# Own tiles for the output halves, and the gate's pieces dealt out anew between the samples' SSD step and their attention

## The chip, the cores and the metric

The kernel runs on one core of a Trainium2 chip. Its engines are TensorE (PE; its weight loads are shown as PEld), VectorE (DVE), ScalarE (ACT), GpSimd (POOL) and SyncE (SP), whose queue issues nearly all transfers here. Each engine works through its own instructions in order; semaphores hold an instruction back until what it reads is there and the buffer that it writes is free. The metric is the device time of one execution in microseconds (us), less is better.

## The reference

One layer of a decoder trunk on a prompt of 2048 tokens and on 8 samples of 4 tokens, d_model 1024, all in float32:

```
h = rmsnorm(x, pre_g);  u = h @ w_in          # 1024 -> 5648 columns
x_lru, g_lru, q, k, v, g_attn, z, xbc, dt_raw = split(u)
y_lru  = rg_lru(causal_conv(x_lru)) * silu(g_lru)          # 512 wide
y_attn = dilated_window_attention(q, k, v) * silu(g_attn)  # 512 wide, 8 heads
y_ssd  = rmsnorm_groups(ssd(causal_conv(xbc), dt) * silu(z)) * ssd_norm_g   # 1024 wide
out = x + rmsnorm(concat(y_lru, y_attn, y_ssd) @ w_out, post_g)
```

The samples continue from caches of keys and values and from an SSD state of 8 x 16 x 64 x 128 numbers, which is read, updated and written back. The new states are outputs too.

## The kernel before

**Products.** Each product with the large weights is made three times over, as high x high, high x low and low x high parts of both operands (`mm3`, L82 to L84). So one column tile of 128 output features over 512 tokens is 8 x 3 = 24 matmuls.

**Stages.** In order: values, keys, queries and the gates; the RG-LRU branch; the convolution of xbc; the SSD step of the samples (`samples`); the attention of the samples over their caches (`sample_part`, dealt out by `fills`); the attention of the prompt (16 units, `attend`); and last the chunkwise SSD of the prompt (`ssd_part`, 16 chunks of 128 tokens) together with the output projection (`out_chunk`, the same 16 chunks, and one for the samples after the eighth).

**The gate z.** Its 1024 columns are eight tiles of 128 (`z_tile`), and a tile is five pieces of 512, 512, 256, 288 and 512 tokens. A piece is 24 matmuls into one of four PSUM buffers (tag "mm"), one SiLU on ACT into one of two buffers zo (L605), and one transfer to the DRAM scratch d_z (L606). A tile begins with the load of its weights (L143), a scaling on POOL (L146), and the split on ACT and DVE (L147, L148). Tiles 0 to 5 are the generator `zs`, 30 pieces, which serve as filler: `samples` yields 20 times and `fills` 80 times, and at some of these points one piece is drawn. What is left over is drawn at the end of `fills`. Tiles 6 and 7 follow in `z_end`, ten pieces, interleaved with the first scores of the prompt's attention. The table preload and all the attention's exponentials on ACT are held behind the last SiLU of `z_end`.

**The samples' SSD step.** For each of two groups there are two rounds of four samples. A round loads four states (tag "h0", two buffers of four states, L793), transposes them on PE (L798), copies them on ACT (L800), multiplies (L804), forms the update on PE (L808, PSUM tag "mm"), adds it on DVE (L810) and writes the states back (L815).

**The chunks.** `out_chunk(c)` makes 32 steps of three matmuls: with 8 row blocks of w_out for the halves 0 and 1, then with the other 8 blocks for both. The first 8 blocks take the RG-LRU and attention outputs, loaded as ym; the other 8 take `chunks[c]`, the high and low parts of the normalised SSD output, which `ssd_part(c)` left. `ssd_part` has 15 steps for each chunk, of which about one is drawn after every two steps of `out_chunk`, so that chunk c + 1 of the SSD runs under chunk c of the output and ends about a quarter into its own. Its steps for each of the two groups g: the decay matrix (load sg, L697 to L700), the transposed x (L710), the products yd and yo (L1251, L1256), the sum y (L1264 to L1267), the squares for the norm (ACT L721, POOL L722 and L723), the update of the state hT, then the sum over partitions on PE (rs, L726), the scaling L730, and the split into sh and sl (L1288, L1289).

**The buffers around the change.** Pool `ck` has two buffers for each tag. The SSD's y (L1264) and the finished output halves ot (L1459, L1460, sent by L1461) share the tag "yt", so they take turns on two buffers; each chunk takes four in the order y of group 0, y of group 1, ot of half 0, ot of half 1, where the y of group 1 of the next chunk comes right behind the two ot. sh and sl are tiles of all 8 blocks, two buffers each.

**Order.** The framework's planner sets each engine's order of instructions: it goes by the place in the program and by its own estimate of when the inputs are ready and buffers free, so an instruction can stand earlier or later than the program has it. On the chip the order is fixed.

Of the kernel before, what the change touches and what calls it, by code (L numbers as in the profile page):

```python
# [8 lines left out]
F32 = mybir.dt.float32  # L9
F32R = mybir.dt.float32r  # L10
AF = mybir.ActivationFunctionType
OP = mybir.AluOpType
# [20 lines left out]
def tile_hybrid_step(ctx: ExitStack, tc: tile.TileContext, A):  # L33
    nc = tc.nc
    act, dve, pool, pe, sp = nc.scalar, nc.vector, nc.gpsimd, nc.tensor, nc.sync
# [45 lines left out]
    def mm3(out, wh, wl, xh, xl, start, stop):  # L81
        pe.matmul(out, lhsT=wh, rhs=xh, start=start, stop=False)  # L82
        pe.matmul(out, lhsT=wh, rhs=xl, start=False, stop=False)  # L83
        pe.matmul(out, lhsT=wl, rhs=xh, start=False, stop=stop)  # L84
# [517 lines left out]
    def z_tile(pl, m):  # L602
        def evac(ps, t0, n):
            zt = pl.tile([128, 512], F32, tag="zo", name="zo", bufs=2)
            z_last.append(act.activation(out=zt[:, :n], in_=ps[:, :n], func=AF.Silu))  # L605
            sp.dma_start(out=d_z[128 * m:128 * m + 128, t0:t0 + n], in_=zt[:, :n])  # L606
        yield from project_steps(C_Z + 128 * m, evac, order=[CHUNKS[i] for i in (2, 1, 3, 4, 0)])
# [124 lines left out]
    def load_z(ck, c, g):  # L732
        return load_rows4(ck, c, g, "zt", d_z)
# [3 lines left out]
    zs = (None for m in range(6) for _ in z_tile(zo, m))  # L737


    with tc.tile_pool(name="cks", bufs=1) as ck:  # L740
        ps = {"t": (psT, "tp"), "y": (psG, "g")}
# [84 lines left out]
                sp.dma_start(out=d_ys[512 * g:512 * g + 512].rearrange("(j p) t -> p j t", p=128), in_=y)  # L826
                yield

        for _ in samples():
            next(zs, None)  # L830

    with tc.tile_pool(name="sa", bufs=1) as sa:
        evac_n = [0]
# [122 lines left out]
                yield  # L956

        for i, _ in enumerate(fills()):
            if i % 3 == 0:
                next(zs, None)  # L960
        for _ in zs:
            pass
# [3 lines left out]
    wo = {}  # L966
# [241 lines left out]
    chunks = {}  # L1208
# [25 lines left out]
    def ssd_part(c):  # L1234
        ck = ck0 if c == 0 else late["ck"]
        ps6 = {"t": (psA, "mm"), "y": (psA, "mm")} if c == 0 else late["ps6"]
        bc, gm, bt = ssd_open(c, ck, ps6, late["tri0" if c == 0 else "tri"])
        yield
        for g in range(2):
            hs = slice(8 * g, 8 * g + 8)  # L1240
            ecB = None if c == 0 else ck.tile([128, 4, 128], F32, tag="ecB", name="ecB", bufs=1)
            sg = ssd_decay(c, g, ck, gm, ecB)
            yield
            xb, xdt, xte = ssd_x(c, g, ck, ps6)
            pool.tensor_tensor(out=xb, in0=xb, in1=dF[:, 4 * g:4 * g + 4, None].to_broadcast([128, 4, 128]), op=OP.mult)
            yield
            hT = late["hT"]
            yd = psA.tile([128, 4, 128], F32, tag="mm", name="yd")
            for m in range(4):
                for e in range(2):  # L1250
                    pe.matmul(yd[64 * e:64 * e + 64, m], lhsT=xdt[:, 2 * m + e], rhs=sg[:, 2 * m + e],  # L1251
                              start=(m == 0), stop=(m == 3), skip_group_check=True)

            yo = None if c == 0 else psA.tile([128, 4, 128], F32, tag="mm", name="yo")
            for m in range(4 if c else 0):
                pe.matmul(yo[:, m], lhsT=hT[:, g, 128 * m:128 * m + 128], rhs=bc[:, 2 + g],  # L1256
                          start=(m == 0), stop=(m == 3), skip_group_check=True)
            yield
            zt = load_z(ck, c, g)
            y = ck.tile([128, 4, 128], F32, tag="yt", name="y")  # L1260
            if c == 0:
                dve.tensor_tensor(out=y, in0=yd, in1=xb, op=OP.add)
            else:
                dve.tensor_tensor(out=y, in0=yo, in1=ecB, op=OP.mult)  # L1264
                dve.tensor_tensor(out=y, in0=y, in1=yd, op=OP.add)
                dve.tensor_tensor(out=y, in0=y, in1=xb, op=OP.add)
            dve.tensor_tensor(out=y, in0=y, in1=zt, op=OP.mult)  # L1267
            yield
            norm = group_norm(ck, ps6, y, 128, dve if c == 0 else pool)
            next(norm)  # L1270
            yield
            stp = psA.tile([128, 512], F32, tag="mm", name="stp")
            pe.matmul(stp, lhsT=bt[:, g], rhs=xte.rearrange("p h d -> p (h d)"), start=True, stop=True)
            if c == 0:
                act.copy(out=hT[:, g], in_=stp)
            else:
                hv = hT[:, g].rearrange("p (h d) -> p h d", d=64)
                pool.tensor_tensor(out=hv, in0=hv, in1=dec[:, c, hs, None].to_broadcast([128, 8, 64]), op=OP.mult)
                dve.tensor_tensor(out=hT[:, g], in0=hT[:, g], in1=stp, op=OP.add)
            yield  # L1280
            for _ in norm:
                pass
            if g == 0:
                mh = ck.tile([128, 8, 128], F32R, tag="sh", name="sh")
                ml = ck.tile([128, 8, 128], F32R, tag="sl", name="sl")
                chunks[c] = mh, ml
            kk = slice(4 * g, 4 * g + 4)
            act.copy(out=mh[:, kk], in_=y)  # L1288
            dve.tensor_tensor(out=ml[:, kk], in0=y, in1=mh[:, kk].bitcast(F32), op=OP.subtract)  # L1289
            yield  # L1290

    ssd = (None for c in range(16) for _ in ssd_part(c))
# [29 lines left out]
    for i in range(16):  # L1322
# [3 lines left out]
        n = [0, 0]  # L1326
# [29 lines left out]
    ck = es.enter_context(tc.tile_pool(name="ck", bufs=2))  # L1356
# [28 lines left out]
    def out_chunk(c):  # L1385
        smp = c == 16
        t0, n = TT[c]
        if not smp:
            mh = c1.tile([128, 8, 128], F32R, tag="mh", name="mh")
            ml = c1.tile([128, 8, 128], F32R, tag="ml", name="ml")  # L1390
            for k0 in (0, 4):
                ym = load_rows4(ck, c, k0 // 4, "ym", d_y, 1)
                kk = slice(k0, k0 + 4)
                act.copy(out=mh[:, kk], in_=ym)
                dve.tensor_tensor(out=ml[:, kk], in0=ym, in1=mh[:, kk].bitcast(F32), op=OP.subtract)
        ops, ots, xres = [], [], []

        def residual(hf):
            sl = slice(512 * hf, 512 * hf + 512)
            xres.append(ck.tile([128, 512], F32, tag="x", name="xres", bufs=2))  # L1400
            src = A["x_prompt"][0, t0:t0 + n, sl] if not smp else A["x_sample"].rearrange("b l d -> (b l) d")[:, sl]
            sp.dma_start(out=xres[hf][:n], in_=src)

        def scaled(hf):

            sl = slice(512 * hf, 512 * hf + 512)
            ots.append(ck.tile([128, 512], F32, tag="yt", name="ot"))
            dve.tensor_tensor(out=ots[hf], in0=ops[hf], in1=pgB[:, sl], op=OP.mult)
            residual(hf)

# [3 lines left out]
        for hf in range(2 if smp else 0):  # L1414

            sl = slice(512 * hf, 512 * hf + 512)
            pq = psA.tile([128, 512], F32, tag="mm", name="pq")
            for k in range(4):
                for i in range(2):
                    for j in range(4):  # L1420
                        kk = 4 * j + k
# [5 lines left out]
            ps = psO.tile([128, 512], F32, tag="o", name="ops")  # L1427
# [5 lines left out]
        for hf, k in () if smp else order:  # L1433
            if cnt[hf] == 0:
                ops.append(psO.tile([128, 512], F32, tag="o", name="ops"))
            ps = ops[hf]
            sl = slice(512 * hf, 512 * hf + 512)
            h_, l_ = (mh, ml) if k < 8 else chunks[c]
            mm3(ps[:n], h_[:, k % 8, :n], l_[:, k % 8, :n], wo[k][0][:, sl], wo[k][1][:, sl],
                cnt[hf] == 0, cnt[hf] == 15)  # L1440
            cnt[hf] += 1
            yield
            if cnt[hf] == 16:
                jk = ck.tile([128, 512], F32, tag="zt", name="jk")
                act.activation(out=jk[:n], in_=ps[:n], func=AF.Square, accum_out=oss[:n, hf:hf + 1])
                if c == 15:
                    scaled(hf)
        dve.tensor_tensor(out=oss[:n, 0:1], in0=oss[:n, 0:1], in1=oss[:n, 1:2], op=OP.add)
        r = rstd_of(sm, oss[:, 0:1], DM, n, "ro")
        for hf in range(2):  # L1450
            sl = slice(512 * hf, 512 * hf + 512)
            dst = A["y_prompt"][0, t0:t0 + n, sl] if not smp else A["y_sample"].rearrange("b l d -> (b l) d")[:, sl]
            if c == 15:
                ot = ots[hf]
                dve.scalar_tensor_tensor(out=ot, in0=ot, scalar=r, in1=xres[hf], op0=OP.mult, op1=OP.add)
            else:
                residual(hf)
                ot = ck.tile([128, 512], F32, tag="yt", name="ot")
                dve.scalar_tensor_tensor(out=ot[:n], in0=ops[hf][:n], scalar=r[:n], in1=pgB[:n, sl], op0=OP.mult, op1=OP.mult)  # L1459
                dve.tensor_tensor(out=ot[:n], in0=ot[:n], in1=xres[hf][:n], op=OP.add)  # L1460
            sp.dma_start(out=dst, in_=ot[:n])  # L1461

    def last_state():
        for g in range(2):
            tp = psT.tile([128, 4, 128], F32, tag="tp", name="tpf")
            for j in range(4):
                pe.transpose(tp[:, j], hT[:, g, 128 * j:128 * j + 128], ident)
            ho = ck.tile([128, 4, 128], F32, tag="ho", name="ho", bufs=1)
            act.copy(out=ho, in_=tp)
            sp.dma_start(out=A["ssd_h_p"][0, 0, 8 * g:8 * g + 8].rearrange("(m e) p n -> (e p) m n", e=2), in_=ho)  # L1470

# [9 lines left out]
    for c in range(16):  # L1481
        k = 0
# [115 lines left out]
```

## Time and profile before

| | |
|---|---|
| median of 3 runs | 2015.51 us (2010.99 to 2017.05) |
| the profiled execution | 2012.49 us |
| its span, first to last instruction | 2010.6 us |
| PE busy | 1925.6 us (96%) |
| DVE busy | 1066.6 us (53%) |
| ACT busy | 742.7 us (37%) |
| POOL busy | 279.2 us (14%) |
| granted TensorE clock, mean | 0.990 of full speed |

The profile is that of one execution. A busy time is the time in which the engine had an instruction at work. Since matmuls overlap, the duration shown for a single matmul (0.39 us for 512 columns) is longer than the distance from one to the next. Waits are named by what ended them.

### The profile page before, as it was taken

To read this page: it belongs to the slowest core of one execution; us is meant where nothing else is said; L and a number is where in the kernel's file an instruction comes from. 1 tells how busy PE (TensorE), PEld (TensorE's weight loads), DVE (VectorE), ACT (ScalarE), POOL (GpSimd) and SP (SyncE) were. 2 spreads that over 40 slices of the span, in tenths; PEclk is the share of its full clock that TensorE was granted. 3 is DMA by queue.
4 is the path that set the end of the run, shared out by engine and by line. 5 is a ranking of instruction groups with operands and counts; after the bars stand their busy time and mean duration, and the time that the engine had idled before them with its cause. 6 is when DMAs were issued, how large, how long until landed. Compare 5 with 4: busy or idle time off the path is not lost.

```text
span 2010.6 us, 35818 instructions
## 1 busy us (share of the span) xinstructions
PE 1925.6 (96%) x14218; PEld 1569.0 (78%) x14218; DVE 1066.6 (53%) x2314; ACT 742.7 (37%) x1464; POOL 279.2 (14%) x346
## 2 busy tenths in 40 slices
PE   7999999999999999999999889999988999989998
PEld 7998888888888888887877667777756777567776
DVE  7315433434323666664223236666767676566664
ACT  6311525252422222223234235556543333333332
POOL 0100101111001111110001000000122232222221
PEclk9999999999999999999999999999999999999999
DMA  8322111111233222225377664334554434234341
GB/s 244 116 75 62 54 54 59 48 61 55 87 93 97 66 73 71 78 69 158 106 208 206 185 176 129 101 102 133 166 157 132 129 112 129 83 108 130 110 126 63
DMA packets 277106, 221.75 MB, mean 110 GB/s; under 512 B 33458, under 2 KB 233122, under 8 KB 276940
## 3 DMA queue, kind: packets, MB, share of 16 engines
q1 hardware_dynamic: 276940, 219.47, 36.2%
q8 instruction: 112, 1.84, 0.4%
q14 instruction: 54, 0.44, 0.1%
HBM read 150.55 MB, written 68.86 MB: 109 GB/s over the span
## 4 chain that ended last, share of the span: by engine, by line
PE 70%; DVE 9%; DMA 8%; ACT 6%; issue 4%; POOL 2%; SPq 1%; DVEq 0%; POOLq 0%; ACTq 0%
PE mm L82 15%; PE mm L83 15%; PE mm L84 15%; PE pt L1142 3%; DMA out_dram<-ot 2%; PE o L1178 2%; ACT sr L1114 2%; PE s L1087 2%; PE ops L83 2%; PE ops L84 2%; PE ops L82 2%; PE s L1066 1%; PE mmt L82 1%; PE mmt L83 1%; PE mmt L84 1%
## 5 line engine op out<-in xcount | busy, mean ns | idle before, releaser
L82 PE MATMUL mm<-xh,wh 128*128 128x512 f32 (+2 forms) x1600 | 563.9, 352 | 0.0
L83 PE MATMUL mm<-xl,wh 128*128 128x512 f32 (+2 forms) x1600 | 560.9, 351 | 0.0
L84 PE MATMUL mm<-xh,wl 128*128 128x512 f32 (+2 forms) x1600 | 560.2, 350 | 0.0
L82 PEld LDWEIGHTS mm<-xh,wh 128*128 128x128 f32 x1600 | 301.6, 188 | 40.7 <-issue 2.9
L83 PEld LDWEIGHTS mm<-xl,wh 128*128 128x128 f32 x1600 | 301.4, 188 | 39.8 <-issue 2.5
L84 PEld LDWEIGHTS mm<-xh,wl 128*128 128x128 f32 x1600 | 300.7, 188 | 38.7 <-issue 1.2
L146 POOL TENSOR_TENSOR wr<-wr,gC 128x1024 f32<-128x1024 f32 x40 | 78.7, 1967 | 398.1 <-DMA wr<-in_w_in_dram 351.4
L439 DVE SCALAR_TENSOR_TENSOR o<-u,ssdc,o 128x512 f32<-128x512 f32 (+1 forms) x216 | 122.8, 590 | 5.1
L148 DVE SCALAR_TENSOR_TENSOR wl<-wr,wh 128x1024 fp32r<-128x1024 f32 x40 | 48.9, 1223 | 120.4 <-ACT wh L147 120.4
L1114 ACT ACTIVATE sr<-sr,nm 128x384 f32<-128x384 f32 (+3 forms) x128 | 97.9, 771 | 23.3 <-DVE nm L1110 14.1
L619 ACT ACTIVATE o<-o 128x512 f32<-128x512 f32 (+2 forms) x60 | 33.1, 552 | 149.9 <-DVE o L439 78.0
L437 DVE TENSOR_SCALAR o<-u,ssdc 128x512 f32<-128x512 f32 (+1 forms) x72 | 47.2, 669 | 65.0 <-ACT u L419 56.8
L1025 ACT COPY ptsb<-pt 128x512 f32<-128x512 f32 x96 | 52.4, 583 | 75.4 <-PE pt L1142 75.3
L82 PE MATMUL mmt<-wh,xh 128*128 128x256 f32 (+3 forms) x272 | 79.2, 293 | 1.0 <-ACT xh L250 0.6
L695 ACT ACTIVATE ecB<-sg 64x512 f32<-64x512 f32 x60 | 37.8, 630 | 113.3 <-DVE y L1264 92.7
L84 PE MATMUL mmt<-wh,xl 128*128 128x256 f32 (+3 forms) x272 | 78.4, 289 | 0.0
L83 PE MATMUL mmt<-wl,xh 128*128 128x256 f32 (+3 forms) x272 | 77.9, 288 | 0.0
L1142 PE MATMUL pt<-ident,sr 128*128 128x128 f32 x576 | 75.2, 281 | 2.3 <-ACT sr L1114 1.8
L1142 PEld LDWEIGHTS pt<-ident,sr 128*128 128x128 f32 x576 | 63.7, 143 | 14.6 <-issue 8.8
L697 DVE TENSOR_SCALAR sg<-sg,cum 128x128 f32<-128x128 f32 (+1 forms) x256 | 70.0, 337 | 5.4 <-ACT ecB L695 5.2
L1087 PE MATMUL s<-k,q 64*32 64x256 f32 (+1 forms) x1536 | 68.9, 348 | 3.8 <-DVE mx L1075 3.2
L1091 DVE CUSTOM_DVE_ANT_0 sr<-s,bias 128x128 f32<-128x128 f32 (+3 forms) x128 | 58.8, 486 | 25.2 <-PE s L1087 24.1
(534 smaller groups left out, 3565.4 us busy)
## 6 DMA issues: line engine op xcount, KB each, us to landing
wr<-in_w_in_dram SPq DMA_DIRECT2D x40, 512.0 KB
sg<-d_cum SPq DMA_DIRECT2D x30, 512.0 KB
d_xbc<-o SPq DMA_DIRECT2D x36, 256.0 KB
x<-in_x_prompt_dram SPq DMA_DIRECT2D x32, 256.0 KB
vt<-in_cache_attn_v_dram SPq DMA_DIRECT2D x32, 256.0 KB
kc<-in_cache_attn_k_dram SPq DMA_DIRECT2D x32, 256.0 KB
xres<-in_x_prompt_dram SPq DMA_DIRECT2D x32, 256.0 KB
out_dram<-ot SPq DMA_DIRECT2D x32, 256.0 KB
```

The lines of the kernel that those rows point to most:

```text
L82: pe.matmul(out, lhsT=wh, rhs=xh, start=start, stop=False)
L83: pe.matmul(out, lhsT=wh, rhs=xl, start=False, stop=False)
L84: pe.matmul(out, lhsT=wl, rhs=xh, start=False, stop=stop)
L146: pool.tensor_tensor(out=wr, in0=wr, in1=gC[:, :, None].to_broadcast([128, 8, 128]), op=OP.mult)
L148: dve.scalar_tensor_tensor(out=wl, in0=wr, scalar=scale, in1=wh.bitcast(F32), op0=OP.mult, op1=OP.subtract)
L439: dve.scalar_tensor_tensor(out=o, in0=v(t), scalar=w[:, t:t + 1], in1=o, op0=OP.mult, op1=OP.add)
L697: dve.tensor_scalar(out=sg[:n, h], in0=sg[:n, h], scalar1=cum[:n, c, 8 * g + h:8 * g + h + 1], scalar2=0.0, op0=OP.subtract, op1=OP.min)
L1025: act.copy(out=out, in_=in_)
L1087: pe.matmul(ps[e][32 * n:32 * n + 32, 256 * h:256 * h + m], lhsT=qr[hd[e], r, 32 * n:32 * n + 32], rhs=krs[h][hd[e], r, 0:m // 32], start= ...
L1091: dve.tensor_tensor_reduce(out=sr[e][r][:, :nk], in0=ps[e][:, :nk], in1=bs[:, e, 512 - nk:512], scale=1.0, scalar=NEG, op0=OP.add, op1=OP. ...
L1114: act.activation(out=sr[e][r], in_=sr[e][r], func=AF.Exp, bias=nm[:, e, r:r + 1], accum_out=ll[:, e, r:r + 1])
L1142: pe.transpose(tp[:, r], sr[e][r][:, 128 * g:128 * g + 128], ident)
```

## The change

There are four edits.

- In `samples`, a piece of z is drawn at two of three yields (14 of 20) instead of at each.
- In `fills`, a piece is drawn at every fifth yield instead of every third, so that the remaining 16 of the 30 pieces are drawn up to the 76th of the 80 yields; before, the remaining 10 were drawn by the 28th.
- The output halves ot get a tag of their own, "ot", with two buffers; "yt" is left to the SSD's y.
- The split SSD output is kept in one tile for each group: two buffers for group 0, one for group 1. The last state's tile ho moves from a tag of its own with one buffer to the tag "x", whose two buffers also hold the residual rows xres.

```diff
@@ -826,8 +826,9 @@
                 sp.dma_start(out=d_ys[512 * g:512 * g + 512].rearrange("(j p) t -> p j t", p=128), in_=y)
                 yield
 
-        for _ in samples():
-            next(zs, None)
+        for i, _ in enumerate(samples()):
+            if i % 3 < 2:
+                next(zs, None)
 
     with tc.tile_pool(name="sa", bufs=1) as sa:
         evac_n = [0]
@@ -956,7 +957,7 @@
                 yield
 
         for i, _ in enumerate(fills()):
-            if i % 3 == 0:
+            if i % 5 == 0:
                 next(zs, None)
         for _ in zs:
             pass
@@ -1280,13 +1281,11 @@
             yield
             for _ in norm:
                 pass
-            if g == 0:
-                mh = ck.tile([128, 8, 128], F32R, tag="sh", name="sh")
-                ml = ck.tile([128, 8, 128], F32R, tag="sl", name="sl")
-                chunks[c] = mh, ml
-            kk = slice(4 * g, 4 * g + 4)
-            act.copy(out=mh[:, kk], in_=y)
-            dve.tensor_tensor(out=ml[:, kk], in0=y, in1=mh[:, kk].bitcast(F32), op=OP.subtract)
+
+            mh, ml = [ck.tile([128, 4, 128], F32R, tag=f"s{i}{g}", name=f"s{i}", bufs=2 - g) for i in "hl"]
+            chunks[c, g] = mh, ml
+            act.copy(out=mh, in_=y)
+            dve.tensor_tensor(out=ml, in0=y, in1=mh.bitcast(F32), op=OP.subtract)
             yield
 
     ssd = (None for c in range(16) for _ in ssd_part(c))
@@ -1404,7 +1403,7 @@
         def scaled(hf):
 
             sl = slice(512 * hf, 512 * hf + 512)
-            ots.append(ck.tile([128, 512], F32, tag="yt", name="ot"))
+            ots.append(ck.tile([128, 512], F32, tag="ot", name="ot"))
             dve.tensor_tensor(out=ots[hf], in0=ops[hf], in1=pgB[:, sl], op=OP.mult)
             residual(hf)
 
@@ -1435,8 +1434,9 @@
                 ops.append(psO.tile([128, 512], F32, tag="o", name="ops"))
             ps = ops[hf]
             sl = slice(512 * hf, 512 * hf + 512)
-            h_, l_ = (mh, ml) if k < 8 else chunks[c]
-            mm3(ps[:n], h_[:, k % 8, :n], l_[:, k % 8, :n], wo[k][0][:, sl], wo[k][1][:, sl],
+            h_, l_ = (mh, ml) if k < 8 else chunks[c, k // 4 - 2]
+            j = k if k < 8 else k % 4
+            mm3(ps[:n], h_[:, j, :n], l_[:, j, :n], wo[k][0][:, sl], wo[k][1][:, sl],
                 cnt[hf] == 0, cnt[hf] == 15)
             cnt[hf] += 1
             yield
@@ -1455,7 +1455,7 @@
                 dve.scalar_tensor_tensor(out=ot, in0=ot, scalar=r, in1=xres[hf], op0=OP.mult, op1=OP.add)
             else:
                 residual(hf)
-                ot = ck.tile([128, 512], F32, tag="yt", name="ot")
+                ot = ck.tile([128, 512], F32, tag="ot", name="ot")
                 dve.scalar_tensor_tensor(out=ot[:n], in0=ops[hf][:n], scalar=r[:n], in1=pgB[:n, sl], op0=OP.mult, op1=OP.mult)
                 dve.tensor_tensor(out=ot[:n], in0=ot[:n], in1=xres[hf][:n], op=OP.add)
             sp.dma_start(out=dst, in_=ot[:n])
@@ -1465,7 +1465,7 @@
             tp = psT.tile([128, 4, 128], F32, tag="tp", name="tpf")
             for j in range(4):
                 pe.transpose(tp[:, j], hT[:, g, 128 * j:128 * j + 128], ident)
-            ho = ck.tile([128, 4, 128], F32, tag="ho", name="ho", bufs=1)
+            ho = ck.tile([128, 4, 128], F32, tag="x", name="ho", bufs=2)
             act.copy(out=ho, in_=tp)
             sp.dma_start(out=A["ssd_h_p"][0, 0, 8 * g:8 * g + 8].rearrange("(m e) p n -> (e p) m n", e=2), in_=ho)
```

## Rows read from the trace of the kernel before

**Rows 1.** Busy time of each engine in stages of the span, granted clock, DMA.

```profile
core 0: us, PE busy (x) PEld busy (x) DVE busy (x) ACT busy (x) POOL busy (x), PEclk, DMA share, GB/s
905.00:1010.00 105.00, 102.56 (x600) 84.64 (x599) 34.82 (x104) 27.60 (x46) 8.98 (x22) 0.97 0.46 137
...
1060.00:1160.00 100.00, 92.44 (x918) 66.56 (x917) 30.82 (x89) 34.94 (x61) 6.73 (x17) 0.98 0.67 186
...
1500.00:1980.00 480.00, 447.26 (x2442) 339.32 (x2441) 325.74 (x601) 168.22 (x344) 136.19 (x144) 0.99 0.38 116
```

**Rows 2.** Who waited for whom, 1500 to 1980 us: total, times, longest.

```profile
PE rs L726 <- POOL sq L723: 30.3, 27, 3.6
...
DVE y L1264 <- DMA out_dram<-ot: 35.4, 11, 5.2
```

**Rows 3.** The chain that ended last, around a chunk: start us, us, what.

```profile
1812.63 0.23 PE ops L82
...
1817.91 3.07 DMA out_dram<-ot
...
1821.10 0.70 DVE y L1264
...
1826.72 0.49 PE rs L726 x2
...
1830.08 0.63 ACT sh L1288
```

**Rows 4.** The timeline of DVE: the first sum of y, group 1, two chunks.

```profile
1787.53 0.69 DVE L1264 TENSOR_TENSOR y<-yo,ecB 128x512 f32<-128x512 f32 x1 [5.25 <-DMA out_dram<-ot]
...
1852.75 0.69 DVE L1264 TENSOR_TENSOR y<-yo,ecB 128x512 f32<-128x512 f32 x1 [2.33 <-DMA out_dram<-ot]
```

**Rows 5.** The timeline of PE: rs of group 1; at 1840.87 of group 0.

```profile
1517.35 0.49 PE L726 MATMUL rs<-sq,ones 128*128 128x128 f32 x2 [2.36 <-POOL sq L723]
...
1793.14 0.49 PE L726 MATMUL rs<-sq,ones 128*128 128x128 f32 x2 [3.56 <-POOL sq L723]
...
1840.87 0.49 PE L726 MATMUL rs<-sq,ones 128*128 128x128 f32 x2 [0.39 <-POOL sq L723]
...
1858.38 0.49 PE L726 MATMUL rs<-sq,ones 128*128 128x128 f32 x2 [0.66 <-POOL sq L723]
...
1988.80 0.49 PE L726 MATMUL rs<-sq,ones 128*128 128x128 f32 x2 [0.32 <-POOL sq L723]
```

**Rows 6.** Stages again: a chunk with a long wait, then a short one.

```profile
1779.62:1815.87 36.25, 32.25 (x169) 25.04 (x168) 23.04 (x43) 11.53 (x23) 9.68 (x10) 0.95 0.36 109
1815.87:1847.80 31.93, 30.57 (x168) 23.81 (x168) 22.88 (x42) 11.44 (x23) 9.69 (x10) 1.00 0.40 125
```

**Rows 7.** The timeline of ACT: SiLUs of z around the stall.

```profile
1104.96 0.60 ACT L605 ACTIVATE zo<-mm 128x512 f32<-128x512 f32 x1
...
1153.76 1.28 ACT L605 ACT_TABLE_LOAD   x1
1155.24 1.25 ACT L605 ACTIVATE zo<-mm 128x512 f32<-128x512 f32 x2 [0.20 <-DMA d_z<-zo]
```

**Rows 8.** The queue of SP: the transfers of z that came late.

```profile
1150.69 0.85 SPq L606 DMA_DIRECT2D d_z<-zo  x2
```

**Rows 9.** Stages of 10 us, end of the samples' attention and behind it.

```profile
1140.00:1150.00 10.00, 6.89 (x93) 3.94 (x91) 4.45 (x13) 3.00 (x7) 0.00 (x0) 1.00 0.72 194
1150.00:1160.00 10.00, 6.78 (x113) 5.16 (x114) 2.27 (x8) 3.84 (x7) 0.00 (x0) 0.83 0.47 135
1160.00:1170.00 10.00, 7.55 (x105) 6.84 (x108) 2.49 (x16) 1.18 (x3) 0.00 (x0) 0.98 0.70 220
1170.00:1180.00 10.00, 10.00 (x77) 6.99 (x62) 2.83 (x18) 1.01 (x2) 0.00 (x0) 0.85 0.74 195
```

**Rows 10.** The queue of SP: the SSD step's last states; their loads.

```profile
954.20 2.02 SPq L793 DMA_DIRECT2D h<-in_state_ssd_h_dram  x4
```

**Rows 11.** The timeline of ACT: the copies of those states, transposed.

```profile
986.19 1.06 ACT L800 COPY h0T<-tph 128x512 f32<-128x512 f32 x2
```

## The prediction

> **What bounds the kernel now.** I read the stages first, then PE's waits, then the chain, then single queues. By the table of the profile PE is busy 96% of the span, so a gain can only come out of 85 us in which PE had nothing, and out of stretches at the lower of its clock levels (1.2 GHz instead of 2.4; a mean of 0.95 over a stretch is a tenth of it at the lower level). The stages [rows 1] show where the 85 us lie and what each part of the change can touch: 32.7 us in the output stage (480 less 447.3), 7.6 us in the samples' attention (1060 to 1160), 2.4 us in the samples' SSD step (905 to 1010). The rest lies at the start, in the prompt's attention and at the end, where the change does nothing. DVE is at 68% in the output stage, so it is no bound by its amount of work, but by when it does it.
>
> In the output stage nearly all of PE's idle time has one name: rs, the sum over partitions for the group norm, waits for POOL's squares, 30.3 of the 32.7 us [rows 2]. The reader is to see that POOL is only the last link. DVE waits 35.4 us in all for the transfer of ot out of the chip before it may write the SSD's next y, since both take turns on "yt" [rows 2]. The chain [rows 3] has it in order: ot goes out (3.07 us), y starts, and 5.6 us later rs does, while PE has stood still.
>
> **The output halves.** The edit takes the wait for the transfer away: y of group 1 then has a buffer whose last use was in the chunk before. No instruction is added; what remains before y are the sums for ot themselves. How much of PE's waits goes? Compare one chunk's pair of waits: DVE 5.25 and PE 3.56 us in one, 2.33 and 0.66 in another [rows 4, 5]. The difference is 1.69 and 1.67: the PE wait follows the transfer one for one, and with the transfer gone y would be there 1.7 us before PE asks. There are 15 such waits of group 1, from 2.36 (first) to 0.32 (last) [rows 5], 22.9 us in sum; group 0, which never waits for ot, has the other 7 us.
>
> But order is planned. If the planner counted some time for that transfer, it will now put rs earlier among PE's matmuls, and eat up the 1.7 us. Bounds: the whole 22.9 goes (order as now), or rs moves up so far that the short chunks keep what they have, some 0.96 each, and only the excess of the six long waits (2.36, 1.85, 2.79, 2.44, 3.56, 2.60) goes, 9.8 us. I take the value of group 0 as what a wait without ot looks like: about 0.4 (0.39 in [rows 5]), with its larger ones 0.5. 15 x 0.5 = 7.5 stay, so 15.4 us go.
>
> After a long wait the clock falls. The chunk with the 3.56 us wait has a clock of 0.95 and 32.25 us of busy PE; the next has 1.00 and 30.57 for one matmul less [rows 6]. That is 1.7 us on top of the wait. Four of the fifteen chunk periods have 0.94 or 0.95: 4 x 1.6 = 6.5 us. Without long waits these go. Sum of this part: -21.9 us, bounds -30 (22.9 + 7) and -16 (9.8 + 6.5).
>
> **The split of sh and sl.** The same two casts and two subtractions for each chunk, in smaller tiles. Group 1 has one buffer, so its write must come after PE's last read in the chunk before. It does now: the chunk ends at about 1815.9, the write starts at 1830.08 [rows 3, 6]. 14 us cover it; without them ACT would stall by what is missing, and with it the exponentials behind the cast. I count nothing. ho on the tag of xres can hold back one transfer or one copy at the very end: at most one transfer like that of ot (3.07, [rows 3]), at least nothing; I take +1.
>
> **The pieces of z.** A piece is 24 matmuls of 0.23 us [rows 3], 5.5 us for 512 tokens, about 2.8 and 3.1 for 256 and 288 (by columns); a tile 22.4. Six pieces, one whole tile and one piece of 512, move from the SSD step into the attention: 28 us of PE work. With them go six SiLUs on ACT, six issues of d_z on SP, and one tile's weight load with its POOL, ACT and DVE passes. On SP they pass the state loads of the SSD step; in the attention, cache loads are queued behind each d_z, and a d_z waits for its SiLU.
>
> What they meet there: now the 30 pieces are all drawn by the 28th of the 80 points, and after that the planner draws pieces of the last two tiles forward. Two SiLUs (the last at 1104.96) fill both zo buffers, and SP issues their transfers only at 1150.69, behind the cache loads; the next two SiLUs run at 1155.24 [rows 7, 8]. The four PSUM buffers are full meanwhile, and PE has no filler: 3.1, 3.2 and 2.4 us idle in three slices, and a clock of 0.83 and 0.85 in two [rows 9]. With pieces, and so d_z, in program order up to the 76th of 80 points, PE has filler up to the end, and the last two tiles' ten pieces (45 us) cover the bias load behind it. I take the idle time of 1060 to 1160 (7.6) and of 1160 to 1170 (2.4) as gone, and 1.7 + 1.5 us of clock: -13.2. Bounds: -13.2, and 0 if the jam only moves.
>
> What they leave: the SSD step, 105 us at 102.6 busy [rows 1], becomes some 77. Does its own chain fit? The last states' loads are issued at 954.20 and copied from 986.19 on [rows 10, 11]: 30 us of slack behind the load. I bound the loss by nothing (planner fills all gaps) and 28 us (the step stays as long as it is). Near the low end: six gaps, each of the length of one of the state copies, some 0.6 us (1.06 for two, [rows 11]): +3.6. Sum of this part: -9.6.
>
> More exponentials now alternate with SiLUs on ACT: two switches for each of the eight parts, 16 where there are 12. A load takes 1.28 us and the SiLU follows 0.2 us behind its end [rows 7]. If all four lay on the path, +5 us. The Trainium skill (ScalarE: Activation LUTs, "What ACT_TABLE_LOAD costs") gives 1283 ns plus a drain of 1380 ns for a switch; by that, four would be +10.6 us and the sum 10.6 us higher. The trace agrees on the load, and shows no such drain here. ACT is busy 35% in that stage [rows 1], and a part's copies have PE's filler over them, so I count nothing and keep +5 as a rival.
>
> **Sum.** -21.9 + 1 - 9.6 = -30.5 against the profiled execution of 2012.5: 1982. The median of the runs is 3 above the profiled one, so I forecast 1985.
>
> **Rivals.**
> - *The next wait takes over* (0.20). rs of group 1 comes after a chain through DVE, ACT and POOL, and group 0's after the loads of ym and sg; if the planner, or these loads, keep PE waiting, the output part gives half of its lower bound, -8. For it: group 0 waits without any ot. Against it: the constant 1.7 us. Time: -8 + 1 - 9.6, about 1999.
> - *Spreading changes nothing* (0.13): the planner has drawn z forward anyway, and jams at the end again. Only -21 of the output part is left: about 1995.
> - *The switches show* (0.07): +5 on the forecast, 1990.
> - *More than that* (0.10): all waits of rs go and all of the clock, -30, and -13 with no loss in the SSD step: about 1973.
> - *The jam repeats, slower* (0.06): d_z stuck on SP behind cache loads that wait for their buffers, as at 1104 to 1150, now at several of the eight parts. The one jam there cost 13.2 us, and the forecast counts it as gone, so it is 1985 + 13.2 for each: from three jams on the kernel is slower (2024.6).
> - *Neither part does anything* (0.06): waits only change names, 2015.
>
> **How the numbers follow.** The forecast has 0.38; its own range, with the bounds of the output part, is 1977 to 1993. The range of 8 in 10 takes in the rivals at 1999, 1995, 1990 and 1973 and leaves out the two at the slow end: 1970 to 2008. 0.3% of this time, about what a measurement can tell from no change, is 6 us. Faster by more: 0.38 + 0.20 + 0.13 + 0.07 + 0.10, less a little for the weak ends: 0.86. The rest goes 0.07 to no change and 0.07 to slower.
>
> **What the profile would show.** Right: no wait of DVE's L1264 for out_dram<-ot; PE's waits for POOL's squares at 10 to 15 us instead of 30; all chunk periods near 31 us, none of 35 or 36, clock 1.00 in them; pieces of z up to the end of the samples' attention, PE busy over 9.5 us in each slice of 10 up to the prompt's attention; the SSD step near 80 us and busy. Wrong: rs of group 1 still waiting 1 us or more in each chunk; ecB or y waiting for sg instead; idle PE between the state transposes of the SSD step; a copy of ho behind the last output.

## The result, and the profile after

The changed kernel takes 1991.98 us (median of 3 runs, 1991.53 to 1994.69) where the kernel before took 2015.51: a ratio of 0.989, 95% interval 0.986 to 0.992. That is 23.5 us faster; the forecast was 1985, with a range of 1970 to 2008. The profiled execution has a span of 1989.8 us where the one before has 2010.6.

The first view is the one that cuts the span into stages, of the kernel after (columns as in [rows 1]).

```profile
905.00:990.00 85.00, 80.79 (x478) 65.21 (x477) 33.43 (x103) 24.47 (x40) 7.29 (x21) 0.94 0.51 150
...
1060.00:1100.00 40.00, 34.12 (x294) 24.15 (x294) 12.16 (x37) 13.87 (x24) 3.66 (x10) 0.87 0.78 218
1100.00:1190.00 90.00, 88.81 (x782) 70.40 (x780) 20.27 (x77) 23.16 (x41) 5.42 (x5) 1.00 0.62 182
...
1500.00:1960.00 460.00, 445.81 (x2457) 339.09 (x2457) 320.81 (x602) 169.20 (x344) 129.07 (x144) 1.00 0.39 122
```

Two things are to be seen beside [rows 1]. The output stage holds the same work in 20 us less: PE was idle for 32.7 of 480 us, and is for 14.2 of 460, at a clock of 1.00. And the stall of [rows 9] is gone (88.8 busy of 90 us, clock 1.00), but another stands at 1060 to 1100, where PE had been busy for 39.4 of 40 us: 5.9 us idle, and a clock of 0.87.

To compare kernels whose stages lie at other times, the table below cuts each profiled span at events that all of them have: the first and the last SiLU of z (the "z stage": SSD step and attention of the samples), and the first and the last scaling of ot. It has the idle time and the mean clock of PE beside each length, from the windows of each run.

| kernel | z stage, us (idle, clock) | first SiLU to first ot | first to last ot, us (idle, clock) | last ot to end |
|---|---|---|---|---|
| before | 281.7 (12.7, 0.98) | 603.1 | 474.0 (32.2, 0.99) | 30.9 |
| after | 283.2 (10.5, 0.96) | 604.2 | 449.8 (13.2, 1.00) | 31.6 |

The output stage gave 24.2 us. The rest, from the first SiLU to the first ot, is 1.1 us longer, the tail 0.7; another 1.6 us lie ahead of the first SiLU, where nothing was changed. A trace is one execution: four kernels with the old dealing, this one before and three of the runs below, have z stages from 276.4 to 281.7 us, so a difference of one or two us there says nothing by itself.

**The wait that is gone.** DVE's timeline after, the same place in a chunk as [rows 4]:

```profile
1801.67 1.41 DVE L1459 SCALAR_TENSOR_TENSOR ot<-ops,rstd,pgB 128x512 f32<-128x512 f32 x2 [0.60 <-ACT rstd L114]
1802.99 1.28 DVE L1460 TENSOR_TENSOR ot<-ot,xres 128x512 f32<-128x512 f32 x2
1804.19 0.68 DVE L1265 TENSOR_TENSOR y<-yo,ecB 128x512 f32<-128x512 f32 x1
```

The first sum of y starts where the second half of ot ends, and its row notes no idle time; before, it stood 5.25 and 2.33 us for the transfer [rows 4]. The view of who waited for whom, 1508.4 to 1958.2 us, has no row of y for out_dram<-ot, and of PE for the squares (total, times, longest; 30.3, 27 and 3.6 in [rows 2]):

```profile
PE rs L726 <- POOL sq L723: 11.9, 19, 2.4
```

The chunks, as in [rows 6]; first the slowest, the second behind the samples' output, then the two that follow it:

```profile
1766.89:1801.67 34.78, 32.32 (x171) 25.46 (x170) 22.95 (x43) 11.55 (x23) 9.22 (x10) 0.95 0.35 114
1801.67:1833.01 31.34, 30.50 (x168) 23.84 (x168) 22.57 (x42) 11.55 (x23) 9.21 (x10) 1.00 0.41 126
1833.01:1863.81 30.80, 30.29 (x166) 23.59 (x166) 22.08 (x43) 11.55 (x23) 8.83 (x10) 1.00 0.41 129
```

**What is late next.** The one long wait that is left, 2.4 us in the slow chunk, shows in the chain of work around it:

```profile
1766.59 6.59 DMA sg<-d_cum
...
1773.26 0.64 ACT ecB L695
...
1774.12 0.70 DVE y L1268
...
1774.90 0.64 ACT sq L721
...
1775.61 0.73 POOL sq L722
1776.42 0.52 POOL sq L723
...
1776.98 0.49 PE rs L726 x2
```

sg has a single tile; its next load starts when the matmuls of yd have read it, and takes 6.6 us here (4.5 in another chunk of the chain). This load is for the next group: the y of this chain does not read it. What holds y is DVE's order, in which the first subtraction in the new sg (L697) stands ahead of y's last factor (L1268):

```profile
1773.92 0.29 DVE L697 TENSOR_SCALAR sg<-sg,cum 128x128 f32<-128x128 f32 x1 [2.04 <-ACT ecB L695]
1774.12 0.68 DVE L1268 TENSOR_TENSOR y<-y,zt 128x512 f32<-128x512 f32 x1
```

ACT, which makes ecB out of sg, shows the same change of what ends last. Before, it stood for y's first sum, which reads the single ecB tile and was itself held up by ot; after, it stands for the load of sg (total, times, longest; before 13.6, 12 and 4.1):

```profile
ACT ecB L695 <- DVE y L1264: 92.7, 14, 8.7
```

```profile
ACT ecB L695 <- DMA sg<-d_cum: 57.5, 22, 6.4
```

**The stall that moved.** Stages of 10 us of the kernel after, then PE's timeline and SP's queue in them:

```profile
1070.00:1080.00 10.00, 9.14 (x101) 5.14 (x99) 3.32 (x11) 2.92 (x7) 0.59 (x3) 1.00 0.56 152
1080.00:1090.00 10.00, 5.69 (x38) 4.20 (x42) 2.12 (x4) 3.66 (x7) 0.00 (x0) 0.56 0.87 241
1090.00:1100.00 10.00, 9.29 (x86) 5.85 (x77) 4.29 (x13) 3.77 (x5) 2.48 (x4) 0.93 0.68 201
```

```profile
1078.75 0.40 PE L84 MATMUL mm<-xh,wl 128*128 128x512 f32 x1
1083.13 1.09 PE L878 MATMUL tp<-ident,kc 128*128 128x128 f32 x4 [3.98 <-DMA kc<-in_cache_attn_k_dram]
...
1095.75 0.50 PE L82 MATMUL mm<-xh,wh 128*128 128x512 f32 x1 [0.36 <-ACT wh L147]
```

```profile
1078.92 0.35 SPq L866 DMA_DIRECT2D sbias<-in_c_sbias_dram  x1
1079.31 2.08 SPq L851 DMA_DIRECT2D kc<-in_cache_attn_k_dram  x4
...
1085.11 0.38 SPq L143 DMA_DIRECT2D wr<-in_w_in_dram  x1
```

A tile of z ends at 1079, and the next one's first matmul comes at 1095.75, since its weights are asked for only at 1085.11. In that gap PE meets the transposes of kc, whose loads stand on SP behind the bias, and the bias waits for its single tile (SP stands 1.2 us ahead of it). Nothing fills the 4 us, and the clock falls to 0.56.

### The profile page after: what moved, and what is told of

Read it like the earlier page. It is cut to its first block, busy times and chain, and to the rows that moved or that the text cites. A ratio compares the mean times of both kernels' runs of the same rounds, so it can differ in the third digit from the quotient of the medians.

```text
span 1989.8 us, 35800 instructions
## 1 busy us (share of the span) xinstructions
PE 1926.7 (97%) x14218; PEld 1569.8 (79%) x14218; DVE 1060.9 (53%) x2314; ACT 746.2 (37%) x1466; POOL 272.0 (14%) x346
## 4 chain that ended last, share of the span: by engine, by line
PE 77%; DMA 6%; DVE 6%; ACT 5%; issue 3%; POOL 2%; SPq 1%; POOLq 0%; ACTq 0%; DVEq 0%
PE mm L84 15%; PE mm L82 15%; PE mm L83 15%; PE ops L83 3%; PE ops L84 3%; PE ops L82 3%; PE pt L1143 3%; PE o L1179 2%; ACT sr L1115 2%; PE s L1088 2%; DMA sg<-d_cum 2%; PE s L1067 1%; PE mmt L82 1%; PE mmt L84 1%; PE mmt L83 1%
## 5 line engine op out<-in xcount | busy, mean ns | idle before, releaser
L1076 DVE CUSTOM_DVE_ANT_1 sr<-s,bias 128x256 f32<-128x256 f32 x128 | 46.5, 420 | 50.2 <-PE s L1067 50.2
L697 DVE TENSOR_SCALAR sg<-sg,cum 128x128 f32<-128x128 f32 (+1 forms) x256 | 68.3, 326 | 7.8 <-ACT ecB L695 7.5
L1092 DVE CUSTOM_DVE_ANT_0 sr<-s,bias 128x128 f32<-128x128 f32 (+3 forms) x128 | 58.7, 486 | 23.9 <-PE s L1088 22.9
```

Source lines behind the costliest of these rows:

```text
L697: dve.tensor_scalar(out=sg[:n, h], in0=sg[:n, h], scalar1=cum[:n, c, 8 * g + h:8 * g + h + 1], scalar2=0.0, op0=OP.subtract, op1=OP.min)
L1092: dve.tensor_tensor_reduce(out=sr[e][r][:, :nk], in0=ps[e][:, :nk], in1=bs[:, e, 512 - nk:512], scale=1.0, scalar=NEG, op0=OP.add, op1=OP. ...
```

## The experiments

Each run was timed beside runs of the kernel before on the same chip, and the ratio is to these. The kernel before took 2015.4 us on the chip of the first four runs, 2016.4 on that of the next three, 2009.1 on that of the next four and 2012.9 on that of the last, so across chips the ratios are to be compared and not the times; the changed kernel has 0.9892. Diffs are against the changed kernel unless said otherwise.

| run | median, us | ratio, 95% interval | z stage, us (idle, clock) | first SiLU to first ot | first to last ot (idle) |
|---|---|---|---|---|---|
| output part alone | 1991.8 | 0.9891 (0.9875 to 0.9907) | 281.5 (12.5, 0.98) | 603.0 | 451.0 (14.4) |
| z part alone | 2011.8 | 0.9994 (0.9978 to 1.0009) | 281.0 (10.1, 0.98) | 603.1 | 471.9 (30.5) |
| split of sh and sl alone | 2015.0 | 1.0002 (0.9988 to 1.0017) | 281.2 (12.3, 0.98) | 599.8 | 477.0 (32.9) |
| y and ot on three tiles | 1994.1 | 0.9904 (0.9886 to 0.9922) | 276.4 (9.9, 0.98) | 598.0 | 452.7 (17.1) |
| weights of z ahead | 1994.5 | 0.9895 (0.9870 to 0.9920) | 283.0 (10.1, 0.96) | 604.2 | 454.1 (17.0) |
| bias behind kc | 2002.5 | 0.9935 (0.9910 to 0.9959) | 287.1 (15.9, 0.97) | 610.6 | 450.9 (16.2) |
| both of these | 1994.7 | 0.9905 (0.9878 to 0.9933) | 281.0 (9.4, 0.98) | 600.5 | 450.5 (14.8) |
| cache rows loaded once | 1988.1 | 0.9883 (0.9853 to 0.9912) | 275.1 (5.0, 0.98) | 599.9 | 453.4 (16.4) |
| the same, z dealt as before | 1975.0 | 0.9816 (0.9782 to 0.9851) | 264.8 (3.7, 0.99) | 588.5 | 449.4 (15.1) |
| one tile for ot | 1998.0 | 0.9929 (0.9901 to 0.9956) | 283.0 (9.7, 0.96) | 606.0 | 454.1 (15.4) |
| squares on DVE | 1994.3 | 0.9916 (0.9890 to 0.9943) | 283.1 (10.1, 0.96) | 601.6 | 455.9 (24.6) |
| z dealt in between | 2003.2 | 0.9950 (0.9931 to 0.9969) | 292.6 (18.3, 0.96) | 615.1 | 451.9 (15.2) |

**The output part alone, and the z part alone.** The two dealings are put back, or only they are changed.

```diff
-        for i, _ in enumerate(samples()):
-            if i % 3 < 2:
-                next(zs, None)
+        for _ in samples():
+            next(zs, None)
...
-            if i % 5 == 0:
+            if i % 3 == 0:
```

> The output part alone (ot on tiles of its own, sh and sl split by group, ho on the tag of xres); z is dealt as in the kernel before. Theory (the whole gain is the output stage's, and the z part gave nothing): first to last ot near 449 us instead of 473, so 1989 to 1992 us, within 3 us of the changed kernel. Rival (the z part gained its forecast 9.6 us and something else lost it): near 2001 us. Rival (the z part cost time by its new stall of PE): 1984 to 1986 us.

> The z part alone: the two dealings of pieces are those of the changed kernel, the output stage is that of the kernel before. Theory (the stall only moved, from 1137 to 1170 us to a boundary of two z tiles): within 3 us of the kernel before, 2012 to 2018 us, with PE waiting for kc at about 1080 us and nothing after 1100 us. Rival (the z part gains as forecast): 2006 us. Rival (it costs): 2018 us or more.

The output part alone is within 0.3 us of the changed kernel. The z part alone is at 0.9994 of the kernel before, with an interval that holds no change. Its trace has the stall of PE at 1080 us (4.9 us for kc) and PE busy without a gap from 1100 to 1170. So the whole gain is the output part's, and the rival that spreading gained and something ate it falls: alone it gains nothing either.

**The split of sh and sl alone.** The output part alone, with ot back on the tiles of y:

```diff
-            ots.append(ck.tile([128, 512], F32, tag="ot", name="ot"))
+            ots.append(ck.tile([128, 512], F32, tag="yt", name="ot"))
...
-                ot = ck.tile([128, 512], F32, tag="ot", name="ot")
+                ot = ck.tile([128, 512], F32, tag="yt", name="ot")
```

> sh and sl split by group and ho on the tag of xres, but ot still shares its tiles with y; z as in the kernel before. Theory (the gain comes from the wait for the transfer of ot alone): the waits of rs stay, 28 to 32 us, and the time is within 4 us of the kernel before. Rival (smaller tiles of sh and sl come free sooner and let the chunks run closer together): half or more of the 24 us, 2003 us or less.

No change, and the waits of the kernel before are all there; from its view of who waited for whom:

```profile
DVE y L1264 <- DMA out_dram<-ot: 44.6, 14, 5.4
...
PE rs L726 <- POOL sq L723: 30.5, 26, 3.7
```

So it is the tile of ot, and not smaller tiles of sh and sl, that gives the time.

**Three tiles for y and ot together.** As that run, with one tile more on the shared tag.

```diff
-            y = ck.tile([128, 4, 128], F32, tag="yt", name="y")
+            y = ck.tile([128, 4, 128], F32, tag="yt", name="y", bufs=3)
...
-            ots.append(ck.tile([128, 512], F32, tag="yt", name="ot"))
+            ots.append(ck.tile([128, 512], F32, tag="yt", name="ot", bufs=3))
...
-                ot = ck.tile([128, 512], F32, tag="yt", name="ot")
+                ot = ck.tile([128, 512], F32, tag="yt", name="ot", bufs=3)
```

> As the run with the split alone, but y and ot share three tiles instead of two, so that the y of group 1 takes the tile of the first half's ot and not that of the second's: a wait for a transfer that started 0.9 us or so earlier. Theory (the wait of PE follows the transfer one for one): the waits of rs shrink by about 1 us for each of 15 chunks and so do the periods, 1995 to 2005 us, between the run with the split alone and the changed kernel. Rival (what counts is that y and ot no longer share a ring at all, since the order is planned by it): nothing gained, 2011 us or more. Rival (any third tile is enough): as the changed kernel's output stage, 1992 us or less.

By its trace the last rival came out: the output stage is 452.7 us, within 3 of the changed kernel's, and y waits for no transfer. (The median, 1994.1, lies between this rival's 1992 and the theory's 1995 and decides nothing.) My expectation had the ring wrong. Tiles are taken in the order y of group 0, both halves of ot, y of group 1. Two tiles gave y of group 1 that of the first half, just sent off; a third gives it that of the y before, and y of group 0, which gets that of the first half, comes some 18 us behind it. One tile is the cure, and a tag of its own is not needed.

**Weights of z ahead, the bias behind kc, and both.** The next tile's weights are loaded when two of five pieces have run; the bias is loaded after the loop over kc and kf.

```diff
-        wh, wl = load_w(c0, scale)
-        for t0, n in order:
+        wh, wl = ahead_w.pop(c0) if c0 in ahead_w else load_w(c0, scale)
+        for i, (t0, n) in enumerate(order):
+            if i == 2 and c_next is not None:
+                ahead_w[c_next] = load_w(c_next)
```

> The changed kernel, with the weights of the next z tile loaded when two pieces of the tile before it have run instead of at the boundary. Theory (PE stalls at 1078 to 1092 us because its filler is missing there: 5.9 us idle between 1060 and 1100 us, and a clock of 0.87 in that stretch, about 4.5 us): both go, 1981 to 1984 us. Rival (kc is late whatever the filler, and the wait stays on PE's in-order queue): 1989 us or more. Rival (the loads now stand before kc on SP's queue and make it later still): 1992 us or more.

> The changed kernel, with the bias of a part loaded behind its kc and kf on SP's queue instead of ahead of them, so that kc no longer waits until the softmax of the part before has given the bias tile back. Theory (this order makes kc late): PE no longer waits for kc, 5.3 us less and the clock with it, 1982 to 1987 us. Rival (kc waits for its own two tiles anyway, or z's weights come late all the same and PE waits for something else): 1990 to 1993 us.

> Both: weights of z ahead, and the bias behind kc. Theory (one stall with two conditions, so either alone takes it away): as the better of the two, 1981 to 1984 us. Rival (two separate losses): lower than either by 3 us or more. Rival (the stall moves on once more): 1989 us or more.

All three theories missed: 1994.5, 2002.5 and 1994.7 where 1981 to 1987 was expected. With the weights ahead the stall at 1080 us is gone, and its like stands 30 us later:

```profile
1060.00:1100.00 40.00, 40.00 (x349) 30.67 (x349) 11.15 (x34) 16.08 (x28) 3.66 (x10) 1.00 0.78 218
1100.00:1140.00 40.00, 33.90 (x313) 23.23 (x312) 12.00 (x33) 13.88 (x24) 3.84 (x5) 0.87 0.60 169
```

With the bias behind kc PE waits less for kc (3.7 instead of 5.3 us), but the next weights are asked for at 1088.71 us, later than before, and PE waits for these, once and long; from its view of who waited for whom, 890 to 1200 us (with both edits it waits 0.9 us for kc, and 3.0 us for the softmax p at 1130 us instead):

```profile
PE mm L82 <- ACT wh L147: 7.3, 1, 7.3
PE tp L876 <- DMA kc<-in_cache_attn_k_dram: 3.7, 3, 3.2
```

**Cache rows loaded once**, with z dealt as after and as before. kc, kf, vt and vf are loaded for the first part and used for all.

```diff
-            vt = [sa.tile([128, 2, 4, 128], F32, tag="vt", name="vt", bufs=3) for _ in range(2)]
...
+            vt, vf = kept["v"], kept["vf"]
...
+                kt_ = kept["k"][i]
```

> The changed kernel with the rows of the cache (kc, kf, vt, vf) loaded for the first of the eight parts alone and used for all of them: leaves out seven eighths of the cache loads, all matmuls stay. Theory (what PE loses in the z stage is lateness of kc behind tiles that are not free yet, wherever the pieces lie): from the first to the last SiLU of z 270 to 274 us instead of 283, so some 10 us less than the changed kernel, 1980 to 1984 us. Rival (the chains over DVE and ACT of a part, or the weights of z, hold PE): 280 us or more in that stage, 1989 us or more.

> The output part alone with the cache rows loaded once, as in the run before: z dealt as in the kernel before. Leaves out the same loads. Theory (both dealings lose the same loads' time, and each would be good without them): within 3 us of the run before, z stage 270 to 274 us. Rival (the stall at the end of the stage is one of z's own, its transfers and SiLUs, and spreading mends it): 280 us in the z stage here, and 6 us or more above the run before.

The stalls between 1060 and 1170 us are gone in both, so the stalls there come of the cache loads, under either dealing: under the new one PE waits for kc itself, under the old one (the output part alone) 4.8 us for the softmax p, without filler. The run takes the loads out of SP's queue as well, so it does not tell their lateness from what they hold up behind them. And the two are not within 3 us: by the ratios the old dealing gains 15 us without the loads (0.9891 to 0.9816), and the new one 2, which is nothing that a measurement can tell (0.9892 to 0.9883). Their z stages, the new dealing first:

```profile
902.10:1177.20 275.10, 270.08 (x2043) 206.25 (x2049) 82.48 (x253) 86.92 (x142) 18.16 (x49) 0.98 0.40 118
```

```profile
902.20:1167.00 264.80, 261.14 (x2042) 206.04 (x2049) 80.66 (x253) 86.29 (x143) 18.00 (x49) 0.99 0.40 117
```

Of the 10.3 us between them 8.9 are busy time, not idle. PE's timeline was added up from the first SiLU to the last, each instruction with the time to the next one's start, less the idle time that the next one notes. The new dealing has 21.0 us in the scores (sc) where the old one has 15.8, and 181.1 in z's own matmuls where the old one has 178.7 (most of that is the clock: 0.74 in 900 to 920 us, and 0.83 in the old one). PE's timeline shows where the scores lose, first the old dealing, then the new:

```profile
1043.28 1.07 PE L895 MATMUL sc<-ktT,qz 128*32 128x512 f32 x8
1044.27 0.50 PE L82 MATMUL mm<-xh,wh 128*128 128x512 f32 x1
```

```profile
1049.30 1.04 PE L896 MATMUL sc<-ktT,qz 128*32 128x512 f32 x2
1050.27 0.66 PE L878 MATMUL tp<-ident,kf 128*128 128x128 f32 x4
1050.86 1.06 PE L896 MATMUL sc<-ktT,qz 128*32 128x512 f32 x6
1051.85 0.50 PE L82 MATMUL mm<-xh,wh 128*128 128x512 f32 x1
```

The four score matmuls of a part write four strips of 32 columns (two records each). All four in a row hold PE for 0.99 us; one by itself and then three hold it for 0.97 and 0.99. In the new dealing other matmuls come between in all eight parts (transposes; in the first part also those of z, which cut it into four); in the old one in five. That is ten cuts against five, and five times 1 us is the 5.2. This is read from the traces; no run changes it alone.

**One tile for ot.**

```diff
-                ot = ck.tile([128, 512], F32, tag="ot", name="ot")
+                ot = ck.tile([128, 512], F32, tag="ot", name="ot", bufs=1)
```

> The changed kernel with one tile for ot instead of two: the second half's first write waits for the transfer of the first half, which is issued some 0.7 us before; y is free of ot, but is queued behind that write on DVE. Theory (the wait for a transfer costs what it exceeds a slack of about 1.7 us by, in each of 15 chunks): a wait of 2.5 to 3 us on DVE gives 0.8 to 1.3 us for each chunk, and the clock with it, 2004 to 2014 us. Rival (only a wait by y itself counts): 1992 us, as the changed kernel. Rival (more than the wait before, because both halves' sums are late): above 2016 us.

Neither: 1998, by the ratio some 7 us above the changed kernel, where the theory has 12 to 22 and the first rival none. The dose did not arrive. DVE's order was planned anew, with y between the halves:

```profile
1806.45 0.75 DVE L1459 SCALAR_TENSOR_TENSOR ot<-ops,rstd,pgB 128x512 f32<-128x512 f32 x1 [0.60 <-ACT rstd L114]
1807.12 0.68 DVE L1265 TENSOR_TENSOR y<-yo,ecB 128x512 f32<-128x512 f32 x1
1807.72 0.73 DVE L1460 TENSOR_TENSOR ot<-ot,xres 128x512 f32<-128x512 f32 x1
...
1812.79 0.74 DVE L1459 SCALAR_TENSOR_TENSOR ot<-ops,rstd,pgB 128x512 f32<-128x512 f32 x1
```

DVE waited for a transfer of ot 2.6 us in all, and the output stage grew by 4.3 us. The run is no measure of the slack; it shows that the planner put another order in the place of such a wait here.

**Squares on DVE.**

```diff
-            norm = group_norm(ck, ps6, y, 128, dve if c == 0 else pool)
+            norm = group_norm(ck, ps6, y, 128, dve)
```

> The changed kernel with the two sums of squares on DVE instead of POOL in all chunks (0.74 and 0.51 us on POOL now). Theory (what is left of the waits of rs, 12 us in 20, is the length of this chain): the chain is 0.6 us shorter or so, most waits of 0.3 to 0.9 us go, 1982 to 1986 us. Rival (the order is planned with the chain's length, or DVE has other work in front): within 3 us of the changed kernel, or slower.

The rival: 1994.3, and PE's idle time in the output stage rises from 13.2 to 24.6 us. PE's waits for the squares stay (12.9 us, now for DVE), though the two sums take 0.70 us there instead of 1.25. Most of the added idle time is a new wait, yd for DVE's xdt: 9.6 us in 13 times. DVE's order changed with the edit, so the run shows that moving the squares there does not pay, and not what sets the waits for them.

**z dealt in between.**

```diff
-            if i % 3 < 2:
+            if i % 6 < 5:
...
-            if i % 5 == 0:
+            if i % 6 == 0:
```

> The changed kernel with a dealing of z between the two: five pieces at each six points of the SSD step instead of two at each three (17 instead of 14), then one piece at each sixth point of the attention instead of each fifth. Theory (what a dealing takes away at one place it gives back at another, since somewhere PE meets a tile that waits for a cache load with no piece of z ready): between 1986 and 1995 us, with an idle stretch of 4 us or more at yet another place between 1060 and 1170 us. Rival (there is a best dealing between the two, with neither the late stall nor the one at 1080 us): 1976 to 1982 us.

Slower than either dealing, and above the theory's 1995: a stall at yet another place, and the longest. PE waits there for kc (2.9 us), p (3.9), kf (2.8) and the weights of z (3.3), one after the other.

```profile
1110.00:1120.00 10.00, 7.46 (x83) 4.21 (x83) 2.64 (x6) 3.80 (x7) 0.00 (x0) 1.00 0.92 254
1120.00:1130.00 10.00, 5.77 (x59) 3.97 (x56) 3.37 (x10) 3.25 (x7) 0.59 (x3) 0.72 0.73 209
1130.00:1140.00 10.00, 5.66 (x61) 2.96 (x59) 2.78 (x9) 1.17 (x2) 0.71 (x1) 0.84 0.53 145
1140.00:1150.00 10.00, 7.64 (x64) 5.24 (x65) 4.21 (x7) 2.78 (x6) 3.08 (x2) 0.59 0.20 54
```

Of the kernels that compute the whole layer, none beats the changed one by more than a measurement can tell.

## Why the prediction was right, and where it was not

- *Output halves, -21.9: right, 24.2 measured.* The idle time fell by 19.0 us (forecast 15.4) and the busy time by 5.2 at the higher clock (forecast 6.5). The pair from which I read 1.7 us was a fair one: in eight of the twelve pairs that the trace before names, DVE's wait is 1.6 to 1.7 us longer than PE's, in the others 0.3 to 1.3. The clock's gain is that of three of the four slow chunks; one is left. The 15 waits of group 1 sum to 9.4 us where I had 7.5. The term that was mis-sized is group 0: I left its 7 us as they were, since it never waits for ot, and they fell to 2.7. No run shows why; the end of ACT's long waits for y is one candidate. The lower bound, that the planner moves rs up and eats the gain, did not come true.
- *Split of sh and sl, 0: right*, by the run of it alone. *Tail, +1: right*, 0.7.
- *z, -9.6: wrong, +1.1 to the first ot, and no change by the run of it alone.* Two of its steps hold. The jam at 1137 to 1170 us [rows 9] is gone: from 1100 to 1190 us PE idles 10 us less, at a clock of 1.00. And the SSD step lost as much as I took, but not as I took it: 4.2 us idle instead of 2.4, and by the clocks (0.94 over 85 us, 0.97 over 105) about 1.9 more. That is 3.7 in sum where I had 3.6, all of it as idle gaps; half of the agreement is luck. The step that failed is "PE has filler up to the end". I counted pieces and their d_z, and named the weight load that goes with each tile of them, but not its lateness: at a boundary of two tiles there is no piece for 16 us, and where kc is late in it, PE stalls. That cost 5.3 us of idle time and 5.2 of clock (0.13 of 40 us) at 1060 to 1100 us, nearly what the jam had cost. My bound "0 if the jam only moves" was the value to take. The time lies in the stated range since the output part alone carries it.
- *Table switches, 0: nothing in the runs speaks against it*; they were not tried by themselves. The attention of the samples has 14 of them after, where I counted on 16 and the kernel before has 12.
- *Two sums.* The bounds of the output part (-30 and -16) put the forecast's own range at 1977 to 1991, not 1993, so the 1992 measured lies just outside it. And "all waits of rs and all of the clock" is 22.9 + 7 + 6.5 = 36.4 by my own terms, not 30.
- *The rivals.* "Spreading changes nothing" (1995, chance 0.13) is nearest to what happened, by another way than the one it named. "The next wait takes over" is there in small: the load of sg behind its single tile, in one chunk.
- *What the profile would show.* Right: no wait of y for ot, 11.9 us of waits for the squares (10 to 15), chunks of 31 us. Wrong: one chunk of 34.8, and 5.7 busy us of 10 at 1080 to 1090 instead of over 9.5. Of my signs of being wrong one is there: ecB waits for sg (57.5 us instead of 13.6). It costs little, since PE's waits fell all the same.

What stays open: why the planner's order under the new dealing parts the scores more often, and whether a dealing exists that meets no late load. Of the dealings and orders tried, each moved the stall.

## What to carry to other kernels

Where two producers take turns on a ring of tiles and one of them is emptied by a transfer, follow the order in which tiles are taken: one more tile may turn a wait for the transfer just issued into one that ended long ago, and here that was worth 24 us of 2015. Here the gain could be read ahead from pairs of waits that rise and fall together in the trace, nearly one for one.

Filler does not remove a late load, it covers it. When filler is dealt out anew, list the loads that are late anyway, and the places where the filler itself has to wait (its own weights), and price the place where the two meet; as long as the load stays late, count the gain as zero.

## What the runs showed of the hardware

Four matmuls of 32 columns into four strips, in a row, took 0.99 us, and one alone 0.97: they run at once if nothing stands between. The Trainium skill (TensorEngine Tiling (Array Packing), Key Properties) says that tiles work independently and can run in parallel, and these traces agree; they show besides that another matmul ahead of the second strip makes PE pay for the first one in full.

A stall of 4 us came with about as much loss by the clock (5.2 us over 40): with 5.7 us of busy PE in the slice from 1080 to 1090 us the granted clock was 0.56, almost the lower of its two levels throughout, and it was 1.00 again from 1100 on.
